# Experts of a mixture-of-experts block: whole steps of neighbouring pairs interleaved, TensorE's order of steps fixed

## The chip, the cores and the metric

The kernel runs on one core of a Trainium2 chip as one launch. The metric is the device time in microseconds (us) from its start to its end; lower is better.

## What is computed

The reference is two transformer blocks in a row on one sequence of 256 tokens with 1024 features, everything in float32. The first block (modulated norms, two kinds of attention, a convolutional feed-forward network) and the attention and convolution part of the second are not touched by the change. What it touches is the last part, a mixture of 32 experts in 4 groups of 8:

```python
y = jnp.zeros_like(h)
for g in range(G):
    hg = jnp.einsum('td,edf->tef', h, w_gate[g])
    hu = jnp.einsum('td,edf->tef', h, w_up[g])
    act = jax.nn.silu(hg) * hu * comb[:, g, :, None]
    y = y + jnp.einsum('tef,efd->td', act, w_down[g])
```

`comb` is zero but for the two experts that a token's router picks in the best group. An expert has a gate and an up matrix of 1024 x 512 and a down matrix of 512 x 1024, 6 MiB together, 192 MiB for all 32.

## The kernel before, in words

The experts are worked through in 16 pairs, by the loop at the end of `moe` (L1604). Each expert has 64 slots for tokens, a pair 128. For one pair the work on the engines is:

- choice: DVE builds `P` (tile `Pm`), a 0/1 matrix of tokens by slots (`onehot`, L1484).
- gather (L1493): TensorE multiplies the normed tokens `hn` by `P`; ScalarE (ACT) copies the result out of PSUM into `xg`. It is called twice for a pair, for half of the features each: once before `experts`, and once after the first quarter of the gate and up products.
- weights of the slots (L1513 to L1520): two small products with `carry`, then five small DVE operations, give `comb`; the choice turned round (L1523, L1525) gives `PTm`.
- gate and up (L1534): 64 matmul instructions, the two experts on the two halves of the array's columns; each fp32 product is two instructions. The weights `we` are loaded from HBM.
- `act` (L1540, L1541): Silu on ACT, then a product with the up result and `comb` on DVE.
- `act` turned (L1544): four transposes on TensorE; ACT copies the result to `aT` (L1546).
- down (L1563): 32 matmul instructions into two PSUM banks `py`, one for each half of the output columns.
- combination (`combine`, L1549): each half is split into a high part `yH` (ACT, L124) and a low part `yL` (DVE, L125); TensorE takes both back to the tokens with `PTm` (L1555, L1556), and DVE adds the result to `acc` (L1558).

The order in which each engine does these things is found by the program's scheduler when the program is built: it knows what depends on what and takes for each engine what is ready and comes earliest in the source. A tile gets a buffer when its first writer is scheduled, and gives it back after its last reader. The pool `tmp4` has two buffers for each tag; `act`, `aT` and `yH` share the tag `act`, and so share two buffers. `xg`, `yL` and `PTm` have one buffer each, `Pm` has two. PSUM is one pool of eight banks.

Weights come by DMA from SyncE's queue (SP, L1366; for the last pair's down matrices L1359), 1 MiB for one load, in the order of use (`eorder`, L1339), into some two dozen buffers that go round; a load starts when TensorE has done with what the buffer held. At the end `more_rounds` (L1635) repeats the work for experts with more than 64 tokens; with these inputs it runs zero times.

Of the kernel before, what the change touches and what calls it, by code (L numbers as in the profile page):

```python
# [20 lines left out]
S = 256  # L21
# [18 lines left out]
# no DMA starts on GpSimd: its ring of descriptors is left small  # L40
# [5 lines left out]
def make_consts():  # L46
# [42 lines left out]
    # for the first block only  # L89
# [14 lines left out]
class Builder:  # L104
# [45 lines left out]
    def wsplit(self, w, name="w"):  # L150
        """-> high and low part"""
        h, l = self.wpart(w.shape, name + "h"), self.wpart(w.shape, name + "l")
        self.split(w, h, l)
        return h, l

    def rsqrt(self, o, v, scale, tmp):
        # o = (v * scale + eps) ** -0.5
        self.nc.scalar.activation(tmp, v, AF.Ln, bias=self.eps[:tmp.shape[0]], scale=scale)
        self.nc.scalar.activation(o, tmp, AF.Exp, scale=-0.5)

    def table(self, name):
        """the set of activation functions for what follows"""
# [79 lines left out]
    def vecs(self):  # L242
        """small vectors, as columns over the partitions"""
# [79 lines left out]
        # -(e0 - e1 + init)  # L323
# [9 lines left out]
    def rope_tables(self):  # L333
# [12 lines left out]
        # wrap into [-pi, pi]  # L346
# [33 lines left out]
    def ada_half(self, pa, w, h):  # L380
        """four column blocks, each on its own columns of the array"""
# [8 lines left out]
    def ada_sum(self, ws):  # L390
        """four column blocks: the row chunks of ws, each times its part of silu(c), summed
        -> [128, 512], to be summed over the partitions"""
# [11 lines left out]
    def ada_ones(self, pa, a, stop=True):  # L404
        """the sum over the partitions, each column block on its own columns of the array"""
# [9 lines left out]
    def ada_cols(self, part):  # L415
        """rows -> columns [128, 4] in psum (without bias), in the order of the pairs"""
# [4 lines left out]
    def ada_load2(self, cols):  # L421
        """two column blocks"""
# [6 lines left out]
    def ada_first(self, w):  # L429
        """-> psum columns [128, 2]; a pair of row chunks on each part of the array"""  # L430
# [14 lines left out]
    def mixer(self):  # L445
# [5 lines left out]
        # small slices of w_in for the rope key and the forget gate, and their padded chunk  # L451
# [6 lines left out]
        # silu(c) as columns, 32 times over  # L458
# [13 lines left out]
        # rms of x, over all partitions  # L472
# [10 lines left out]
        # x, feature-major  # L483
# [41 lines left out]
        def ada(k):  # L525
            """scale and shift for chunks k, k + 1 of h; for one chunk if k < 2"""
# [86 lines left out]
        # --- fox q, k; latent q, kv: times gain, split; the row scale comes later  # L613
# [47 lines left out]
        # token-major sums for the value rows  # L661
# [3 lines left out]
        # --- forget gate, rope key  # L665
# [29 lines left out]
        # --- mla q, k, v  # L695
# [60 lines left out]
        # --- attention, with other products between its steps  # L756
# [23 lines left out]
        def values(kind, j, PT):  # L780
            """two heads, each on half of the array"""
# [14 lines left out]
        def gate(kind, n8):  # L796
            """a chunk of a gate"""
# [15 lines left out]
        # rest of adaLN: the mixer's gate; shift and scale of the ffn; its gate  # L813
# [3 lines left out]
        def ada_rest(n):  # L817
            """the sums over row chunks of four column blocks"""
# [16 lines left out]
        def out_prod(kind, i):  # L835
            """chunks 2i, 2i+1 of a branch's output"""
# [86 lines left out]
    def out_steps(self, wsrc, aH, aL, each, order=(0, 1, 2, 3)):  # L923
        """[D, D] product, feature-major; the last two k chunk by chunk, so that the results come one by one"""
# [17 lines left out]
    def softmax(self, sc):  # L942
        """psum scores [q, 384] (rows of the two query tiles) -> probabilities"""
# [12 lines left out]
    def turn_p(self, P):  # L956
        """blocks (q0,k0) (q1,k0) (q1,k1), turned"""
# [8 lines left out]
    def times_v(self, PTs, what):  # L966
        """o [n, 256] = v^T P^T, for each P and (v, column, n, o)"""
# [8 lines left out]
    def ffn_up(self, g):  # L976
        """parts of the weights of group g, gate and value"""
# [90 lines left out]
    def w2a_load(self, n):  # L1068
        """loads of the first n slices of w_in_2, columns of q, k, v"""
# [13 lines left out]
    def block2(self):  # L1083
# [6 lines left out]
        # sums for both norms; x2 * gains, split  # L1090
# [8 lines left out]
        def norms():  # L1099
# [9 lines left out]
            # eps / s_^2, for the sum over 64  # L1109
# [29 lines left out]
        # products out of psum  # L1139
# [9 lines left out]
        def group_sums(b):  # L1149
            """b [128, 2, S] -> sums of squares over groups of 64, in psum"""  # L1150
# [6 lines left out]
        def group_rms(pg, scaled):  # L1157
            """(mean square + eps / s_^2) ** -0.5, or without s_"""
# [9 lines left out]
        # convolution branch: xc, b, c  # L1168
# [26 lines left out]
        # row scale of v, token-major  # L1195
# [90 lines left out]
        def router(k):  # L1286
            """logits of groups and experts, and the sum of squares, feature by feature"""
# [5 lines left out]
        def router_w():  # L1293
            """router weights, times the gain of their norm"""
# [14 lines left out]
        for j in range(6):  # L1309
# [8 lines left out]
            if j == 2:  # L1318
                # output of the first block, the residual
# [31 lines left out]
    def prefetch(self, n):  # L1351
        for _ in range(n):
            e, nm, hf = key = self.eorder[self.enext]
            if nm == "down" and e == NE - 2:
                # for the last pair by halves of the columns, in turns
# [19 lines left out]
    def route(self):  # L1375
# [25 lines left out]
        # group: first largest, and its probability  # L1401
# [23 lines left out]
        e = self.e = col(2, 2)      # [tile, k]  # L1425
# [4 lines left out]
        # place of a token in its expert's list  # L1430
# [11 lines left out]
        rk = self.rk = col(2, 2)     # [tile, k], from 1  # L1442
# [5 lines left out]
        # weights of the two  # L1448
# [5 lines left out]
        def rest():  # L1454
# [5 lines left out]
            # w split, and the first choice, to be carried to the slots  # L1460
# [6 lines left out]
            # rounds beyond the first  # L1467
# [7 lines left out]
    def slots(self, u):  # L1475
        """u = 64 * expert + place if the place is in 1..64, else 0, of the places in rk"""
# [3 lines left out]
        # rk (rk - 65) is below zero for the places 1..64 only  # L1480
# [3 lines left out]
    def onehot(self, P, u, n):  # L1484
        """P [token, tile, slot]"""
# [7 lines left out]
    def gather(self, xg, P, n, half):  # L1493
        nc = self.nc
        mm = nc.tensor.matmul
        for cc in range(4 * half, 4 * half + 4, 2):
            b = self.bank((128, 2, n))
            for i in range(2):
                for t in range(2):
                    mm(b[:, i], self.hn[:, t, cc + i], P[:, t].bitcast(F32), start=(t == 0), stop=(t == 1),  # L1500
                       skip_group_check=True)
            nc.scalar.copy(xg[:, cc:cc + 2], b)  # L1502

    def experts(self, load, xg, P, first, acc, carry, each=None):
        """one pair of experts over 128 slots; adds to acc [token, tile, D].
        first: the pair's first expert, to compare with the carried one; each: what to do with a tile of
        tokens and half of the columns of acc, if the weights come by such halves"""
        nc, tmp, c = self.nc, self.tmp, self.c
        mm = nc.tensor.matmul
        # weight of a slot; slots to tokens  # L1510
        pw = self.bank()
        for t in range(2):
            mm(pw[:, 0:6], P[:, t], carry[:, t], start=(t == 0), stop=(t == 1))  # L1513
# [5 lines left out]
        comb = tmp.tile([128, 1], F32, name="comb")  # L1519
        nc.vector.scalar_tensor_tensor(a[:, 2:4], a[:, 0:2], 1.0, a[:, 5:7], op0=OP.mult, op1=OP.mult, accum_out=comb)  # L1520
        pp = self.bank((128, 2, 128), F32R)
        for t in range(2):
            nc.tensor.transpose(pp[:, t], P[:, t], self.identr)  # L1523
        PT = tmp.tile([128, 2, 128], F32R, name="PTm", bufs=1)
        nc.vector.tensor_copy(PT, pp.bitcast(F32))  # L1525
        ps = []
        for nm in ("gate", "up"):
            b = self.bank()
            for hf in range(2):
                w = [load(j, nm, hf) for j in range(2)]  # L1530
                for k in range(4):
                    kk = 4 * hf + k
                    for j in range(2):
                        mm(b[64 * j:64 * j + 64], xg[:, kk, 64 * j:64 * j + 64], w[j][:, k], start=(kk == 0),  # L1534
                           stop=(kk == 7), skip_group_check=True)
                if nm == "gate" and hf == 0:
                    self.gather(xg, P, 128, 1)
            ps.append(b)
        act = tmp.tile([128, 512], F32, name="act", tag="act")
        nc.scalar.activation(act, ps[0], AF.Silu)  # L1540
        nc.vector.scalar_tensor_tensor(act, ps[1], comb, act, op0=OP.mult, op1=OP.mult)  # L1541
        pt = self.bank((128, 4, 128))
        for f in range(4):
            nc.tensor.transpose(pt[:, f], act[:, f * 128:(f + 1) * 128], self.ident)  # L1544
        aT = tmp.tile([128, 4, 128], F32, name="aT", tag="act")
        nc.scalar.copy(aT, pt)  # L1546
        py = [self.bank() for _ in range(2)]

        def combine(n):  # L1549
            yH = tmp.tile([128, 512], F32R, name="yH", tag="act")  # L1550
            yL = tmp.tile([128, 512], F32R, name="yL", bufs=1)
# [128 lines left out]
```

## Time and profile before

| | |
|---|---|
| time, median of 3 runs | 1044.03 us (1042.81 to 1044.26) |
| span of the profiled execution, first to last instruction | 1041.6 us |
| time of that execution on its own | not given; the 2.4 us between the span and the median are taken as outside the span |
| mean granted TensorE clock | 0.993 |
| TensorE busy | 987.6 us, 95% |
| VectorE (DVE) busy | 515.3 us, 49% |
| ScalarE (ACT) busy | 371.9 us, 36% |
| experts' stage | from about 558 us to the end |

The span is the time between the first and the last instruction of one execution that the profiler recorded. Busy shares are means over stages with quite different limits. The chain of waits follows the work that ended last back to what released it. A TensorE row of the timeline counts to the modelled end of a matmul, so its rows overlap; the chain's rows do not.

### The profile page before, as it was taken

The numbers are of one execution on the slowest core, as the hardware profiler recorded it, in microseconds if no ns is written. First come the engines' busy times: TensorE is split into PE (matmuls) and PEld (weight loads), VectorE is DVE, ScalarE is ACT, GpSimd is POOL, SyncE is SP. The second block draws the span as 40 slices with busy tenths as digits, with TensorE's granted clock in tenths as the row PEclk, the third lists the DMA queues.
The fourth block names the chain that finished last, engine by engine and source line by source line (L and its number), as shares of the span: only waits on it lengthen the run. The fifth ranks groups of instructions, "written<-read, shape, count | busy, mean of one in ns | idle before, by whom it ended". The sixth has DMA issues, their size and how long they took to land.

```text
span 1041.6 us, 16242 instructions
## 1 busy us (share of the span) xinstructions
PE 987.6 (95%) x6676; PEld 709.1 (68%) x6676; DVE 515.3 (49%) x1004; ACT 371.9 (36%) x652; POOL 27.1 (3%) x25
## 2 busy tenths in 40 slices
PE   6999999999999999999998999999999999999996
PEld 5899999989999999898975443434444444344442
DVE  4868998759876675559744222112222222122121
ACT  3556656638554643656633111111111111111110
POOL 1010000010000000500000000000000000000000
PEclk8999999999999999999999999999999999999999
DMA  9977888539945555272859999999999999999901
GB/s 319 343 279 259 296 272 307 174 102 368 302 162 187 184 203 191 88 228 92 285 184 362 422 418 415 425 419 424 418 423 419 421 424 420 424 417 424 366 1 42
DMA packets 113350, 310.20 MB, mean 298 GB/s; under 512 B 9554, under 2 KB 59128, under 8 KB 96888
## 3 DMA queue, kind: packets, MB, share of 16 engines
q1 hardware_dynamic: 113182, 309.09, 78.1%
q8 instruction: 54, 0.88, 0.3%
q14 instruction: 24, 0.20, 0.1%
q10 hardware_dynamic: 90, 0.03, 0.0%
HBM read 308.05 MB, written 1.05 MB: 297 GB/s over the span
## 4 chain that ended last, share of the span: by engine, by line
PE 90%; DVE 4%; ACT 3%; issue 1%; DMA 0%; POOL 0%; SPq 0%; DVEq 0%; ACTq 0%; POOLq 0%
PE bank L1534 22%; PE bank L129 12%; PE bank L131 12%; PE bank L130 12%; PE bank L1563 11%; PE bank L1500 6%; PE bank L1555 2%; PE bank L1556 2%; DVE act L1541 1%; ACT wh L124 1%; PE bank L1544 1%; DVE wl L125 1%; ACT aT L1546 1%; PE g L129 1%; PE g L130 1%
## 5 line engine op out<-in xcount | busy, mean ns | idle before, releaser
L1534 PE MATMUL bank<-we,xg 128*64 128x512 f32 x1024 | 226.8, 595 | 0.0
L1534 PEld LDWEIGHTS bank<-we,xg 128*64 128x64 f32 x1024 | 70.7, 137 | 131.0 <-issue 127.3
L1563 PE MATMUL bank<-we,aT 128*64 128x512 f32 x512 | 115.1, 596 | 10.8 <-ACT aT L1546 10.8
L129 PE MATMUL bank<-fH,wh 128*128 128x256 f32 x352 | 99.5, 283 | 2.1 <-ACT fH L997 2.1
L130 PE MATMUL bank<-fL,wh 128*128 128x256 f32 x352 | 99.6, 283 | 0.0
L131 PE MATMUL bank<-fH,wl 128*128 128x256 f32 x352 | 99.5, 283 | 0.1
L1563 PEld LDWEIGHTS bank<-we,aT 128*64 128x64 f32 x512 | 38.9, 137 | 75.7 <-issue 60.5
L1541 DVE SCALAR_TENSOR_TENSOR act<-bank,comb,act 128x512 f32<-128x512 f32 x16 | 12.0, 751 | 157.1 <-PE bank L1534 157.1
L125 DVE TENSOR_TENSOR yL<-bank,yH 128x512 fp32r<-128x512 f32 x32 | 22.0, 688 | 131.7 <-ACT yH L124 131.7
L1500 PEld LDWEIGHTS bank<-Pm,hn 128*128 128x128 f32 x512 | 63.3, 192 | 15.6 <-issue 13.0
L1502 ACT COPY xg<-bank 128x256 f32<-128x256 f32 x64 | 23.9, 373 | 127.9 <-PE bank L1500 127.6
L129 PEld LDWEIGHTS bank<-fH,wh 128*128 128x128 f32 x352 | 67.5, 192 | 2.5 <-ACT fH L997 2.5
L131 PEld LDWEIGHTS bank<-fH,wl 128*128 128x128 f32 x352 | 67.5, 192 | 0.3 <-DVE wl L125 0.3
L130 PEld LDWEIGHTS bank<-fL,wh 128*128 128x128 f32 x352 | 67.6, 192 | 0.0
L1500 PE MATMUL bank<-Pm,hn 128*128 128x128 f32 x512 | 66.7, 278 | 0.0
L124 ACT CAST yH<-bank 128x512 fp32r<-128x512 f32 x32 | 18.8, 586 | 109.4 <-PE bank L1563 109.4
L125 DVE TENSOR_TENSOR wl<-wup,wh 128x2048 fp32r<-128x2048 f32 x22 | 50.3, 2289 | 10.6 <-ACT wh L124 10.6
L1546 ACT COPY aT<-bank 128x512 f32<-128x512 f32 x16 | 9.4, 586 | 125.4 <-PE bank L1544 125.4
L1558 DVE TENSOR_TENSOR acc<-acc,bank 128x512 f32<-128x512 f32 x64 | 41.1, 684 | 20.9 <-PE bank L1556 20.9
L130 PE MATMUL bank<-aL,wh 128*128 128x256 f32 x176 | 49.5, 283 | 0.0
L131 PE MATMUL bank<-aH,wl 128*128 128x256 f32 x176 | 49.5, 283 | 0.0
L129 PE MATMUL bank<-aH,wh 128*128 128x256 f32 x176 | 48.9, 283 | 0.0
(449 smaller groups left out, 2165.8 us busy)
## 6 DMA issues: line engine op xcount, KB each, us to landing
we<-in_w_exp_gate SPq DMA_DIRECT2D x64, 1024.0 KB
we<-in_w_exp_up SPq DMA_DIRECT2D x64, 1024.0 KB
we<-in_w_exp_down SPq DMA_DIRECT2D x60, 1024.0 KB
wup<-in_w_up SPq DMA_DIRECT2D x22, 1024.0 KB
wa<-in_w_ada SPq DMA_DIRECT2D x16, 1024.0 KB
wdn<-in_w_down SPq DMA_DIRECT2D x11, 1024.0 KB
wa<-in_w_ada SPq DMA_DIRECT2D x16, 512.0 KB
wgt<-in_w_in SPq DMA_DIRECT2D x8, 1024.0 KB
```

The source lines that it names most:

```text
L124: self.hi = self.nc.scalar.copy(hi, raw)
L125: self.nc.vector.tensor_sub(lo, raw, hi)
L129: mm(o, lh, rh, start=start, stop=False, skip_group_check=True)
L130: mm(o, lh, rl, start=False, stop=False, skip_group_check=True)
L131: return mm(o, ll, rh, start=False, stop=stop, skip_group_check=True)
L1500: mm(b[:, i], self.hn[:, t, cc + i], P[:, t].bitcast(F32), start=(t == 0), stop=(t == 1), skip_group_check=True)
L1502: nc.scalar.copy(xg[:, cc:cc + 2], b)
L1534: mm(b[64 * j:64 * j + 64], xg[:, kk, 64 * j:64 * j + 64], w[j][:, k], start=(kk == 0), stop=(kk == 7), skip_group_check=True)
L1541: nc.vector.scalar_tensor_tensor(act, ps[1], comb, act, op0=OP.mult, op1=OP.mult)
L1555: mm(b, PT[:, t], yH, start=True, stop=False)
L1558: nc.vector.tensor_add(o, o, b)
L1563: mm(py[n][64 * j:64 * j + 64], aT[:, ff, 64 * j:64 * j + 64], w, start=(ff == 0), stop=(ff == 3), skip_group_check=True)
```

## The change

The function `experts`, which did a whole pair, is cut into steps: `gate_up`, `weigh` (weights of the slots), `activate`, `turn_act`, `down`, `parts` (the split of one half), `combine` (one half) and `back` (the choice turned round). The gather of a pair becomes one step, `cols`. The loop then runs through the steps of two neighbouring pairs: gate and up of pair p; the whole gather of pair p+1; the first half of the combination of pair p-1; the transposes of pair p; the weights of the slots of pair p+1; the second half of the combination of pair p-1; the choice of pair p turned round; down of pair p. `step` puts each TensorE instruction of a step behind the last one of the step before (`issue_after`); the other engines' order is left to the scheduler. In `down` the last four products run by halves of the columns, so that the first bank is complete sooner. `combine` takes both high parts, then both low parts. For the last pair the first half is combined between the down products. The rest of the diff takes comments out, and `more_rounds` calls the new functions one after the other.

```diff
-    def gather(self, xg, P, n, half):
+    def gather(self, P):
...
-        for cc in range(4 * half, 4 * half + 4, 2):
-            b = self.bank((128, 2, n))
+        xg = self.tmp.tile([128, KD, 128], F32, name="xg", bufs=1)
+        for cc in range(0, KD, 2):
+            b = self.bank((128, 2, 128))
...
-                if nm == "gate" and hf == 0:
-                    self.gather(xg, P, 128, 1)
...
+    def activate(self, pair):
+        nc = self.nc
+        act = pair["act"] = self.tmp.tile([128, 512], F32, name="act", tag="act")
+        pg, pu = pair.pop("ps")
+        nc.scalar.activation(act, pg, AF.Silu)
+        nc.vector.scalar_tensor_tensor(act, pu, pair["comb"], act, op0=OP.mult, op1=OP.mult)
...
+        pair["aT"] = self.tmp.tile([128, 4, 128], F32, name="aT", tag="act")
+        nc.scalar.copy(pair["aT"], pt)
...
+                        f, n = (i // 2, i % 2) if hf == 0 else (i % 2, i // 2)
+                        last = one(2 * hf + f, n, j, w[j][:, f, n * 512:(n + 1) * 512])
...
+    def parts(self, pair, n):
+        yH = self.tmp.tile([128, 512], F32R, name="yH", tag="act")
+        yL = self.tmp.tile([128, 512], F32R, name="yL", bufs=1)
+        self.split(pair["py"][n], yH, yL)
+        pair[n] = yH, yL
+
+    def combine(self, pair, n, each=None):
+
+        nc, PT, acc = self.nc, pair["PT"], self.acc
+        if n not in pair:
+            self.parts(pair, n)
+        bs = [self.bank() for _ in range(2)]
+        for i, y in enumerate(pair.pop(n)):
+            for t in range(2):
+                last = nc.tensor.matmul(bs[t], PT[:, t], y, start=(i == 0), stop=(i == 1))
+        for t in range(2):
+            o = acc[:, t, n * 512:(n + 1) * 512]
+            nc.vector.tensor_add(o, o, bs[t])
...
+        def step(f, *a):
+
+            with ExitStack() as st:
+                if at[0]:
+                    st.enter_context(tc.issue_after(at[0].ins))
+                at[0] = f(*a)
...
-        for p in range(NE // 2):
-            pair(p, store if p == NE // 2 - 1 else None)
+        select(0)
+        step(cols, 0)
+        self.route_rest()
+        for p in range(np_):
+            q, last = pairs[p], p == np_ - 1
+            load = lambda j, nm, hf: self.expert_w(2 * p + j, nm, hf)
+            if not last:
+                select(p + 1)
+            step(self.gate_up, q, load)
+            if p == 0:
+                step(self.weigh, q, 0)
+            self.activate(q)
+            if p:
+                self.parts(pairs[p - 1], 0)
+            if not last:
+                step(cols, p + 1)
+            if p:
+                step(self.combine, pairs[p - 1], 0)
+            step(self.turn_act, q)
+            if not last:
+                step(self.weigh, pairs[p + 1], 2 * p + 2)
+            if p:
+                step(self.combine, pairs.pop(p - 1), 1)
+            step(self.back, q)
+            if last:
+                def halves(n, i, mm):
+                    at[0] = mm
+                    if n and i == 0:
+                        step(self.combine, q, 0, store)
+                    if i:
+                        self.parts(q, n)
+                step(self.down, q, load, halves)
+                step(self.combine, q, 1, store)
+            else:
+                step(self.down, q, load)
```

## Rows read from the trace of the kernel before

**Rows 1.** The page: TensorE's busy time and share; the chain's shares by engine.

```profile
PE 987.6 (95%) x6676; PEld 709.1 (68%) x6676; DVE 515.3 (49%) x1004; ACT 371.9 (36%) x652; POOL 27.1 (3%) x25
...
PE 90%; DVE 4%; ACT 3%; issue 1%; DMA 0%; POOL 0%; SPq 0%; DVEq 0%; ACTq 0%; POOLq 0%
```

**Rows 2.** Chain of waits through pair 14: start us, us, what.

```profile
974.88 3.58 PE bank L1534 x16
978.47 1.98 PE bank L1500 x16
980.45 10.47 PE bank L1534 x48
991.00 0.76 DVE act L1541
991.81 0.67 PE bank L1544 x4
992.50 0.59 ACT aT L1546
993.14 7.14 PE bank L1563 x32
1000.28 0.66 PE bank L1555 x2
1000.94 0.61 PE bank L1556 x2
1001.55 0.47 PE bank L1555 x2
1002.02 1.56 PE bank L1500 x14
1003.58 0.47 PE bank L1556 x2
1004.05 0.22 PE bank L1500 x2
1004.27 0.12 PE bank L1513 x2
1004.39 0.22 PE bank L1523 x2
1004.61 3.58 PE bank L1534 x16
```

**Rows 3.** Chain of waits: first gate products of the first and the second pair.

```profile
558.54 3.58 PE bank L1534 x16
...
588.26 3.58 PE bank L1534 x16
```

**Rows 4.** Waits from 600 to 1041 us: total us, times, longest.

```profile
PE bank L1544 <- DVE act L1541: 14.2, 15, 1.0
...
PE bank L1563 <- ACT aT L1546: 10.1, 15, 0.7
```

**Rows 5.** Timeline: ACT and DVE work of the combination and the Silu.

```profile
999.46 0.59 ACT L124 CAST yH<-bank 128x512 fp32r<-128x512 f32 x1 [6.37 <-PE bank L1563]
...
1000.07 0.69 DVE L125 TENSOR_TENSOR yL<-bank,yH 128x512 fp32r<-128x512 f32 x1 [8.32 <-ACT yH L124]
...
1001.36 1.29 DVE L1558 TENSOR_TENSOR acc<-acc,bank 128x512 f32<-128x512 f32 x2 [0.59 <-PE bank L1556]
...
1013.81 0.60 ACT L1540 ACTIVATE act<-bank 128x512 f32<-128x512 f32 x1 [3.22 <-PE bank L1534]
```

**Rows 6.** Timeline: issue of the last loads, and the last down products.

```profile
967.51 12.37 SPq L1359 DMA_DIRECT2D we<-in_w_exp_down  x8
...
1030.50 1.94 PE L1563 MATMUL bank<-we,aT 128*64 128x512 f32 x8
```

**Rows 7.** Windows: length, PE, PEld, DVE, ACT, POOL, clock, DMA share, GB/s.

```profile
919.44:949.19 29.75, 28.12 (x147) 12.97 (x146) 6.78 (x18) 3.85 (x8) 0.00 (x0) 1.00 1.02 420
...
979.90:990.00 10.10, 10.10 (x51) 3.70 (x52) 0.00 (x0) 1.03 (x3) 0.00 (x0) 1.00 0.74 273
```

More of the change, by code (lines that the diff above doesn't have):

```diff
@@ L1491, in onehot, with weigh @@
             nc.vector.scalar_tensor_tensor(P[:, t], io, u[:, t, 1:2], p1, op0=OP.is_equal, op1=OP.add)
-    def gather(self, xg, P, n, half):
+    def gather(self, P):
         nc = self.nc
-        mm = nc.tensor.matmul
-        for cc in range(4 * half, 4 * half + 4, 2):
-            b = self.bank((128, 2, n))
+        xg = self.tmp.tile([128, KD, 128], F32, name="xg", bufs=1)
+        for cc in range(0, KD, 2):
+            b = self.bank((128, 2, 128))
             for i in range(2):
                 for t in range(2):
-                    mm(b[:, i], self.hn[:, t, cc + i], P[:, t].bitcast(F32), start=(t == 0), stop=(t == 1),
-                       skip_group_check=True)
+                    last = nc.tensor.matmul(b[:, i], self.hn[:, t, cc + i], P[:, t].bitcast(F32), start=(t == 0),
+                                            stop=(t == 1), skip_group_check=True)
             nc.scalar.copy(xg[:, cc:cc + 2], b)
-    def experts(self, load, xg, P, first, acc, carry, each=None):
-        nc, tmp, c = self.nc, self.tmp, self.c
-        mm = nc.tensor.matmul
+        return xg, last
+    def weigh(self, pair, first):
+        nc, tmp, c, P = self.nc, self.tmp, self.c, pair["P"]
         pw = self.bank()
         for t in range(2):
-            mm(pw[:, 0:6], P[:, t], carry[:, t], start=(t == 0), stop=(t == 1))
+            last = nc.tensor.matmul(pw[:, 0:6], P[:, t], self.carry[:, t], start=(t == 0), stop=(t == 1))
         a = tmp.tile([128, 8], F32, name="cw")
@@ L1518, in experts, with back, gate_up @@
         nc.vector.tensor_scalar(a[:, 6:7], a[:, 4:5], float(-first), c["eslot"], op0=OP.add, op1=OP.not_equal)
-        comb = tmp.tile([128, 1], F32, name="comb")
-        nc.vector.scalar_tensor_tensor(a[:, 2:4], a[:, 0:2], 1.0, a[:, 5:7], op0=OP.mult, op1=OP.mult, accum_out=comb)
+        pair["comb"] = tmp.tile([128, 1], F32, name="comb")
+        nc.vector.scalar_tensor_tensor(a[:, 2:4], a[:, 0:2], 1.0, a[:, 5:7], op0=OP.mult, op1=OP.mult,
+                                       accum_out=pair["comb"])
+        return last
+    def back(self, pair):
+        nc, P = self.nc, pair["P"]
         pp = self.bank((128, 2, 128), F32R)
         for t in range(2):
[L1523 to L1526, printed above, removed]
+            last = nc.tensor.transpose(pp[:, t], P[:, t], self.identr)
+        pair["PT"] = self.tmp.tile([128, 2, 128], F32R, name="PTm", bufs=1)
+        nc.vector.tensor_copy(pair["PT"], pp.bitcast(F32))
+        return last
+    def gate_up(self, pair, load):
+        mm = self.nc.tensor.matmul
+        pair["ps"] = []
         for nm in ("gate", "up"):
@@ L1533, in experts @@
                     for j in range(2):
-                        mm(b[64 * j:64 * j + 64], xg[:, kk, 64 * j:64 * j + 64], w[j][:, k], start=(kk == 0),
-                           stop=(kk == 7), skip_group_check=True)
-                if nm == "gate" and hf == 0:
-                    self.gather(xg, P, 128, 1)
[L1538 to L1541, printed above, removed]
+                        last = mm(b[64 * j:64 * j + 64], pair["xg"][:, kk, 64 * j:64 * j + 64], w[j][:, k],
+                                  start=(kk == 0), stop=(kk == 7), skip_group_check=True)
@@ L1542, in experts, with turn_act @@
+            pair["ps"].append(b)
+        return last
+    def activate(self, pair):
[4 more added lines that the diff above has]
+        nc.vector.scalar_tensor_tensor(act, pu, pair["comb"], act, op0=OP.mult, op1=OP.mult)
+    def turn_act(self, pair):
+        nc, act = self.nc, pair.pop("act")
         pt = self.bank((128, 4, 128))
         for f in range(4):
-            nc.tensor.transpose(pt[:, f], act[:, f * 128:(f + 1) * 128], self.ident)
@@ L1545, in experts @@
[L1545 to L1551, printed above, removed]
-            self.split(py[n], yH, yL)
-            for t in range(2):
-                b = self.bank()
-                mm(b, PT[:, t], yH, start=True, stop=False)
-                mm(b, PT[:, t], yL, start=False, stop=True)
-                o = acc[:, t, n * 512:(n + 1) * 512]
-                nc.vector.tensor_add(o, o, b)
-                if each:
-                    each(t, n)
@@ L1562, in down, with one @@
-        def down(ff, n, j, w):
-            mm(py[n][64 * j:64 * j + 64], aT[:, ff, 64 * j:64 * j + 64], w, start=(ff == 0), stop=(ff == 3),
-               skip_group_check=True)
+            last = nc.tensor.transpose(pt[:, f], act[:, f * 128:(f + 1) * 128], self.ident)
+        pair["aT"] = self.tmp.tile([128, 4, 128], F32, name="aT", tag="act")
+        nc.scalar.copy(pair["aT"], pt)
+        return last
+    def down(self, pair, load, halves=None):
+        aT, py = pair["aT"], [self.bank() for _ in range(2)]
+        pair["py"] = py
+        def one(ff, n, j, w):
+            return self.nc.tensor.matmul(py[n][64 * j:64 * j + 64], aT[:, ff, 64 * j:64 * j + 64], w, start=(ff == 0),
+                                         stop=(ff == 3), skip_group_check=True)
@@ L1566, in experts @@
         for hf in range(2):
             w = [load(j, "down", hf) for j in range(2)]
-            if each:
-                for ff in range(4):
-                    for j in range(2):
-                        down(ff, hf, j, w[j][:, ff])
-                continue
-            for f in range(2):
-                for n in range(2):
-                    for j in range(2):
-                        down(2 * hf + f, n, j, w[j][:, f, n * 512:(n + 1) * 512])
-        for n in range(2):
-            combine(n)
+            for i in range(4):
+                for j in range(2):
+                    if halves:
+                        last = one(i, hf, j, w[j][:, i])
+                    else:
+                        f, n = (i // 2, i % 2) if hf == 0 else (i % 2, i // 2)
+                        last = one(2 * hf + f, n, j, w[j][:, f, n * 512:(n + 1) * 512])
+                if halves and i % 2:
+                    halves(hf, i // 2, last)
@@ new lines, in down @@
+        return last
+    def parts(self, pair, n):
[14 more added lines that the diff above has]
+            nc.vector.tensor_add(o, o, bs[t])
+            if each:
+                each(t, n)
+        return last
@@ L1614, in moe, with select @@
         self.prefetch(NW + NS + NN + 1)
-        def pair(p, each=None):
+        np_ = NE // 2
+        pairs = {}
+        def select(p):
             u = tmp.tile([128, 2, 2], F32, name="ug")
@@ L1620, in pair, with cols @@
             self.onehot(P, u, 128)
-            xg = tmp.tile([128, KD, 128], F32, name="xg", bufs=1)
-            self.gather(xg, P, 128, 0)
-            if p == 0:
-                self.route_rest()
-            self.experts(lambda j, nm, hf: self.expert_w(2 * p + j, nm, hf), xg, P, 2 * p, acc, self.carry, each)
+            pairs[p] = {"P": P}
+        at = [None]
+        def step(f, *a):
[3 more added lines that the diff above has]
+                at[0] = f(*a)
+        def cols(p):
+            pairs[p]["xg"], last = self.gather(pairs[p]["P"])
+            return last
         out = self.out.rearrange("o (t p) d -> (o p) t d", p=128)
@@ L1630, in store @@
             nc.sync.dma_start(out[:, t, 512 * n:512 * n + 512], acc[:, t, 512 * n:512 * n + 512])
-        for p in range(NE // 2):
-            pair(p, store if p == NE // 2 - 1 else None)
+        select(0)
[31 more added lines that the diff above has]
+                step(self.combine, q, 1, store)
+            else:
+                step(self.down, q, load)
         self.more_rounds(store)
@@ L1648, in more_rounds @@
                 self.onehot(P, u, 128)
-                xg = tmp.tile([128, KD, 128], F32, name="xg", bufs=1)
-                self.gather(xg, P, 128, 0)
+                q = {"P": P, "xg": self.gather(P)[0]}
                 def load(j, nm, hf):
@@ L1656, in load @@
                     return w
-                self.experts(load, xg, P, 0, acc, carry)
+                self.weigh(q, 0)
+                self.gate_up(q, load)
+                self.activate(q)
+                self.turn_act(q)
+                self.down(q, load)
+                self.back(q)
+                for n in range(2):
+                    self.combine(q, n)
                 nc.vector.tensor_scalar_add(u, u, -128.0)
```

## The prediction

> **What bounds the kernel now.** I read the page first: TensorE (PE) is busy for 95% of the span and carries 90% of the chain of waits [rows 1]. That looks as if nothing could be had, but a share is a mean, so I went to the chain of one expert pair, which is the stretch that the change rewrites. From one pair's first gate product to the next pair's is 29.73 us, 974.88 to 1004.61 [rows 2], and the 14 pairs from 588.26 to 1004.61 take 29.74 us each [rows 2, 3]. In it the reader should find four places where PE does not stream. After the gate and up products end at 990.92 the chain goes through VectorE (DVE, `act`) and PE starts again at 991.81: 0.89 us. After the four transposes it goes through ScalarE (ACT, `aT`), 992.48 to 993.14: 0.66 us. The four transposes take 0.67 us although two like ones (L1523) take 0.22 us in the stream, so 0.44 us would do: 0.23 us. The first half of the combination takes 0.66 + 0.61 us where the second half, whose inputs are ready, takes 0.47 + 0.47: 0.33 us. The waits of PE confirm the first two: 14.2 us and 10.1 us over 15 pairs, and nothing longer stands there [rows 4]; PE never waits for a load in this stage.
>
> So PE's own sequence bounds the stage, with 0.89 + 0.66 + 0.23 + 0.33 = 2.11 us a pair that isn't streaming. The profile gives a span of 1041.6 us and no separate time for that execution; the median of the runs is 1044.03 us, so I make the sum against the span and add 2.4 us at the end.
>
> **The change, part by part.** Moved without a price of their own: the gather's two halves become one (1.98 + 1.56 + 0.22 = 3.76 us before and after), the slot weights (0.12 us) and the transposes of the choice (0.22 us) change place [rows 2]. The choice itself on DVE comes earlier, beside the gate products, where DVE has nothing else to do; if that cover went, PE would wait about one DVE operation for it, 0.7 us by `yL` [rows 5]. No load is moved past another on SP's queue: `eorder` and the cycle of slots are the same, a load only starts when PE lets go of a slot sooner. The new order of the eight down products (0.22 us each at 7.14 us for 32 instructions) lets the first output bank finish sooner; it costs nothing in itself.
>
> Removed, if everything is ready when PE asks: `act` now has the gather and half a combination (3.76 + 0.94 us) to hide its 0.60 + 0.76 us; `aT` (0.59 us) has 0.12 + 0.94 + 0.22 us; the first half of the parts, `yH` and `yL` (0.59 + 0.69 us [rows 5]), has a whole gate and up stretch of 3.58 + 10.47 us. All four losses go, and a pair takes 29.73 - 2.11 = 27.62 us. That is one end, a gain of 2.11 us a pair.
>
> **The wait that comes instead.** The tiles `act`, `aT` and both `yH` share one tag in a pool of two buffers (L1525, L1540, L1546 and the new `parts`). In the old order two were enough, since a pair finished its `yH` before the next pair's `act`. Now the combination of pair p-1 lies on both sides of pair p's transposes, and three of these tiles are wanted at about one time. The change fixes PE's order only; which tile takes the free buffer is left to the program's scheduler. I see two orders, and price both from the same rows [rows 2, 5].
>
> (A) `act` of pair p gets its buffer during the gate products; the second `yH` gets none before the transposes have read `act`. Behind the last transpose: 0.23 us until its result is out, 0.02 + 0.59 us `aT`, 0.02 + 0.59 us `yH`, 0.04 us to PE: 1.49 us, of which the slot weights hide 0.12 us: 1.37 us idle. `yL` ends another 0.69 us after `yH`, PE takes it up about 0.06 us later, and the `yH` products cover 0.47 us: 0.26 us more. Together 1.63 us; a pair takes 27.62 + 1.63 = 29.25 us.
>
> (B) The second `yH` takes the buffer as soon as `aT` of the pair before is done with, and `act` waits until the first half of the combination has read the first `yH`. From that half's start: 0.66 us for the two `yH` products, 0.04 + 0.60 us for the Silu [rows 5], DVE meanwhile in its first addition from about 1.01 to 1.66 us (0.54 us behind the `yL` products' start, 1.29 us for two), then 0.76 us for `act`, transposes at about 2.48 us against 0.94 us without a wait: 1.54 us. The second addition and `yL` come after `act`, and the `yL` products wait 0.33 us for them. Together 1.87 us; a pair takes 29.49 us. Behind the waiting Silu stand only copies that PE does not want yet; PE itself is who waits.
>
> The other end of this unknown wait is (C) below, 2.85 us. I take A and B, because the two-buffer tag is in the code and both ways round it stalls, and they lie close together.
>
> **The sum.** The first gate product now starts at 558.54 [rows 3]. It moves back by the other half of the gather, 1.78 us, less the weights and transposes that move behind it, 0.34 us: 560.0. The first pair has no combination to do: 14.05 + 0.12 + 3.76 + 0.44 + 0.12 + 0.22 + 7.14 = 25.85 us, to 585.85 (588.26 now [rows 3]). Fourteen pairs follow: by A 14 x 29.25 = 409.5 us, to 995.4. The last pair has no gather and no next weights (29.25 - 3.76 = 25.49 us with the cover of 0.12 us gone) and 0.94 us of its own combination between its down products: 26.4 us, to 1021.8. Now the last down product ends at 1030.50 + 1.94 = 1032.44 [rows 6]. What is behind it stays. A: 10.6 us less, a span of 1031.0 and a time of 1033.4. B by the same working: 998.7, 1025.4, 7.0 us less, a time of 1037. My forecast is 1034 us, faster by 1%; its own range is 1027 to 1042 us.
>
> **Are the loads in the way?** Every pair needs 12 loads of 1 MiB, 12.58 MB. In one pair's time the DMA engines are fully busy and move 420 GB/s [rows 7], which makes 29.95 us a pair, no less than PE takes now. The Trainium skill, HBM Reference, section Specifications (TRN2), says that a core streaming alone comes to about 425 GB/s, bounded by its DMA engines; 12.58 MB at that rate is an estimate of 29.6 us a pair, by which the stage could not get shorter and the time would stay near 1044. The rows speak against it: the last eight loads are issued from 967.51 on [rows 6] and the traffic ends inside the stretch to 990.0 (273 GB/s mean, 0.74 busy) [rows 7], while PE uses the last of them at 1030.50 [rows 6]. PE is some 40 us behind the loads. So the transfers hold the end to about 990 + 1.9 + 9.2 us (last products and tail) = 1001 us, not to 1044, and all the gain of A, B and even of the full 2.11 us fits into the lead.
>
> **The rivals.** *Full gain*: the scheduler finds an order in which the second `yH` takes the first one's buffer right at the combination, and nothing stalls. Then 585.85 + 14 x 27.62 = 972.5, the last pair 27.62 - 3.88 + 0.94 = 24.7 us, 997.2: 35.2 us less, 1008.8 us. For it: PE's order gives each step enough cover. Against: two buffers. *Slower* (C): as B, but DVE takes both additions and `yL` ahead of `act`: 1.01 + 1.29 + 0.69 + 0.76 + 0.04 = 3.79 us from the half's start, a wait of 2.85 us. A pair then takes 30.47 us; 560.0 + 25.85 + 14 x 30.47 = 1012.4, the last pair 27.7 us, 1040.1: 7.7 us more, 1051.7 us. It decides as soon as the new wait is over some 2.3 us (2.11 us a pair and the first pair's 2.4 us spread over 14). For it: DVE takes its work in one order, and two of these are ready before the Silu ends. Against: `act` comes earlier in the program. *Loads bind*: as weighed above, no change, 1044 us; it needs the lead to be gone, and the rows show 40 us of it.
>
> **How the numbers follow.** A change under 0.2% (about 2 us) can't be told from none here. A or B 0.50, full gain 0.25, slower 0.17, loads bind 0.08. A small part of B's spread reaches no change or above. So faster 0.75, same 0.09, slower 0.16. The range takes in A, B, the full gain with some 4 us for the unseen edges, and no change: 1005 to 1046 us; it leaves out nearly all of C.
>
> **What would show it.** Right: the waits of PE for `act` and `aT` gone or nearly; the gather in one piece of about 3.8 us; a pair of about 29.3 us; a new wait of PE for `yH` (A) or for `act` with the Silu behind the combination (B), 1.4 to 1.9 us. Full gain: no wait of PE over 0.2 us and pairs of 27.6 us. C: transposes waiting over 2.3 us. Loads: PE waiting for `we`. I would be wrong if the first half of the combination kept its 1.27 us, or if the gather or the transposes cost more in their new places than the rows of before say.

## The result and the profile after

The changed kernel takes 1024.16 us (median of 4 runs, 1023.10 to 1024.95) against 1044.07 us for the kernel before (4 runs): a ratio of 0.9815, 95% interval 0.9801 to 0.9828, 19.9 us less. The forecast was 1034 us with a range of 1005 to 1046. So the direction was right and the time lies in the range, 10 us below the forecast. It lies outside the narrower range of 1027 to 1042 us that went with cases A and B; the wide range holds it because it takes in the full gain.

On the page of the changed kernel TensorE (PE) and the chain look almost as before [rows 1]:

```profile
PE 978.9 (96%) x6676; PEld 707.6 (69%) x6676; DVE 515.2 (50%) x1004; ACT 368.8 (36%) x652; POOL 27.1 (3%) x25
...
PE 92%; ACT 3%; DVE 2%; DMA 1%; issue 1%; POOL 0%; SPq 0%; DVEq 0%; ACTq 0%; POOLq 0%
```

A share can't show the change: the same instructions are there in a shorter time. The chain of waits through one pair does; these are its pieces (start us, us, what), and they answer to [rows 2]:

```profile
815.49 13.73 PE bank L1544 x64
829.23 3.77 PE bank L1501 x32
833.00 0.93 PE bank L1601 x4
833.92 0.45 PE bank L1560 x4
...
834.40 0.59 ACT aT L1562
834.98 0.50 ACT yH L124
...
835.52 1.47 PE bank L1601 x4
836.99 0.12 PE bank L1529 x2
837.12 7.02 PE bank L1571 x32
844.13 1.28 PE bank L1544 x5
```

A pair takes 844.13 - 815.49 = 28.64 us instead of 29.73 us. The reader should see four things. The product on VectorE (DVE) for `act` is no longer on the chain. `aT` still is, but not because the down products wait for it: ScalarE (ACT) does `aT` and then the second `yH`, and it is the second half of the combination (L1601 at 835.52) that waits for that `yH`. The four transposes take 0.45 us and not 0.67 us. And the 64 gate and up products take 13.73 us in one piece, where they were 3.58 + 10.47 = 14.05 us.

The waits of PE from 600 us to the end (total us, times, longest) say the same; the two lines of [rows 4], 24.3 us together, are gone, and one of 16.5 us stands in their place:

```profile
PE bank L1601 <- ACT yH L124: 16.5, 16, 1.2
```

On the timeline of ACT and DVE (start, us, engine, line, operation) the order is that of case A in the prediction: `aT` first, the second `yH` behind it, `yL` behind that:

```profile
834.40 0.59 ACT L1562 COPY aT<-bank 128x512 f32<-128x512 f32 x1 [0.99 <-PE bank L1560]
834.88 0.59 ACT L124 CAST yH<-bank 128x512 fp32r<-128x512 f32 x1
...
835.50 0.69 DVE L125 TENSOR_TENSOR yL<-bank,yH 128x512 fp32r<-128x512 f32 x1
...
835.52 0.73 PE L1601 MATMUL bank<-yH,PTm 128*128 128x512 f32 x2 [1.04 <-ACT yH L124]
```

The loads end where they ended before. In the windows of [rows 7] (length, PE, PEld, DVE, ACT, POOL, clock, DMA share, GB/s) one pair's DMA is as busy as it was, and the traffic still ends at about 990; but PE now uses the last load at 1011.69 and not at 1030.50 [rows 6]:

```profile
815.49:844.13 28.64, 27.60 (x147) 12.70 (x144) 6.84 (x19) 3.64 (x8) 0.00 (x0) 1.00 1.02 425
...
979.50:990.00 10.50, 10.50 (x50) 3.86 (x52) 1.62 (x3) 0.00 (x0) 0.00 (x0) 1.00 0.83 306
```

```profile
1011.69 1.94 PE L1571 MATMUL bank<-we,aT 128*64 128x512 f32 x8
```

PE's lag behind the loads fell from some 40 us to some 22 us.

### The profile page after: what moved, and what is told of

It is laid out like the page before. It is cut to its first block, busy times and chain, and to the rows that moved or that the text cites. A ratio compares the mean times of both kernels' runs of the same rounds, so it can differ in the third digit from the quotient of the medians.

```text
span 1022.8 us, 16189 instructions
## 1 busy us (share of the span) xinstructions
PE 978.9 (96%) x6676; PEld 707.6 (69%) x6676; DVE 515.2 (50%) x1004; ACT 368.8 (36%) x652; POOL 27.1 (3%) x25
## 4 chain that ended last, share of the span: by engine, by line
PE 92%; ACT 3%; DVE 2%; DMA 1%; issue 1%; POOL 0%; SPq 0%; DVEq 0%; ACTq 0%; POOLq 0%
PE bank L1544 21%; PE bank L129 13%; PE bank L130 13%; PE bank L131 13%; PE bank L1571 11%; PE bank L1501 6%; PE bank L1601 4%; ACT aT L1562 1%; PE g L129 1%; ACT yH L124 1%; PE g L130 1%; PE g L131 1%; PE bank L1560 1%; ACT wh L124 1%; PE bank L970 1%; PE bank L961 1%
## 5 line engine op out<-in xcount | busy, mean ns | idle before, releaser
L1544 PE MATMUL bank<-we,xg 128*64 128x512 f32 x1024 | 222.5, 592 | 0.0
L1544 PEld LDWEIGHTS bank<-we,xg 128*64 128x64 f32 x1024 | 73.5, 137 | 145.7 <-issue 144.4
L1553 ACT ACTIVATE act<-bank 128x512 f32<-128x512 f32 x16 | 9.6, 597 | 237.7 <-PE bank L1544 237.7
L1571 PEld LDWEIGHTS bank<-we,aT 128*64 128x64 f32 x512 | 35.3, 137 | 65.3 <-issue 63.5
L1501 PEld LDWEIGHTS bank<-Pm,hn 128*128 128x128 f32 x512 | 59.4, 195 | 11.5 <-issue 11.5
L1501 PE MATMUL bank<-Pm,hn 128*128 128x128 f32 x512 | 62.4, 281 | 0.0
L124 ACT CAST wh<-wup 128x2048 fp32r<-128x2048 f32 x22 | 41.8, 1902 | 14.0 <-PE bank L130 13.3
```

The costliest lines, as they stand in the source:

```text
L124: self.hi = self.nc.scalar.copy(hi, raw)
L1501: last = nc.tensor.matmul(b[:, i], self.hn[:, t, cc + i], P[:, t].bitcast(F32), start=(t == 0), stop=(t == 1), skip_group_check=True)
L1544: last = mm(b[64 * j:64 * j + 64], pair["xg"][:, kk, 64 * j:64 * j + 64], w[j][:, k], start=(kk == 0), stop=(kk == 7), skip_group_check=True)
L1571: return self.nc.tensor.matmul(py[n][64 * j:64 * j + 64], aT[:, ff, 64 * j:64 * j + 64], w, start=(ff == 0), stop=(ff == 3), skip_group_ch ...
```

## The experiments

The theory after the result: the change hides `act`, `aT` and the breaks between products of different shape, and pays for it with a wait for the second `yH`, which has no buffer until the transposes have read `act`. Its rivals: the wait is ScalarE's serial work whatever the buffers; the gain comes from the combination's place, or from the fixed order as such; the loads set the end. All runs below are compared with the kernel before on the same chip; its medians there were 1043.8 and 1043.7 us.

**Sharing the two buffers out differently.**

```diff
-        act = pair["act"] = self.tmp.tile([128, 512], F32, name="act", tag="act")
+        act = pair["act"] = self.tmp.tile([128, 512], F32, name="act", tag="act", bufs=1)
...
-        yH = self.tmp.tile([128, 512], F32R, name="yH", tag="act")
+        yH = self.tmp.tile([128, 512], F32R, name="yH", tag="yH", bufs=1)
```

(`aT` has the tag `act` with one buffer too, and two small tiles of the router are given one tag each.)

> The changed kernel with the same memory shared out differently: act and aT share one buffer, yH has one of its own, instead of all three sharing two. The second yH can then start when the first half of the combination has read the first one, before the transposes. Buffer theory: the 1.04 us for which TensorE waits for the second yH in each pair goes; but yL then stands behind two additions on VectorE (1.29 us) and becomes what TensorE waits for, some 0.6 us, so a pair takes about 28.2 us against 28.64, and the time falls by 5 to 7 us to about 1018. Rival (the wait is ScalarE's serial work, aT then yH, whatever the buffers): the wait stays at 1.0 us and the time at 1024.

Measured: 1016.79 us (1016.39 to 1017.41), ratio 0.9742 (0.9726 to 0.9758). With the same memory the wait for `yH` is gone but for one in the last pair; what is left is a wait for `yL`, 0.7 us a time. The chain of one pair shows why (start us, us, what): `yL` stands behind the two additions of the first half.

```profile
880.73 3.77 PE bank L1501 x32
884.50 0.72 PE bank L1601 x3
...
885.24 1.28 DVE acc L1604 x2
...
886.60 0.61 DVE yL L125
...
887.25 0.73 PE bank L1601 x2
```

A pair takes 895.12 - 866.99 = 28.13 us. So it was the buffer: ACT's work is the same and PE no longer waits for it.

**The gather behind the transposes.**

```diff
-            if not last:
-                step(cols, p + 1)
             if p:
                 step(self.combine, pairs[p - 1], 0)
             step(self.turn_act, q)
             if not last:
+                step(cols, p + 1)
                 step(self.weigh, pairs[p + 1], 2 * p + 2)
```

> The changed kernel with two steps exchanged and no more memory: the first half of the combination stands right behind the gate and up products, then the transposes, then the whole gather of the next pair, then the rest. The gather (3.77 us) then covers aT, the second yH and its yL. Buffer theory: no wait of TensorE over 0.2 us is left, a pair takes 13.73 + 0.94 + 0.45 + 3.77 + 0.12 + 0.94 + 0.22 + 7.02 = 27.2 us, the time falls by about 14 x 1.4 + 1 = 20 us to 1004. Loads theory: the last load lands at 990 in both kernels, so the end can't come before about 1001, and TensorE begins to wait for weights in the last pairs; then 1004 to 1010. Rival (the steps cost more in other places): 1015 or more.

Measured: 1007.60 us (1007.49 to 1010.00), ratio 0.9661 (0.9645 to 0.9677). This beats both kernels, the changed one by 16.6 us. Its chain through one pair has nothing but PE in it (two short steps of 0.12 us are left out here):

```profile
805.38 13.73 PE bank L1544 x64
819.11 1.13 PE bank L1601 x4
820.24 0.44 PE bank L1560 x4
820.68 3.57 PE bank L1501 x32
...
824.37 1.04 PE bank L1601 x4
...
825.53 7.02 PE bank L1571 x32
832.55 1.71 PE bank L1544 x7
```

A pair takes 832.55 - 805.38 = 27.17 us, as expected. The time is 3.6 us above my 1004, inside what the loads theory allowed, but 1.5 us of that are not the loads: the first pair takes 588.10 - 560.50 = 27.60 us against 26.08 us in the changed kernel, since it has no combination and no gather ahead of its transposes, and PE waits 1.8 us for its `act`. The last pair has no gather, so there PE waits 1.16 us for the second `yH` again, and it waits for weights for the first time in this stage (from the timeline, the last 14 up products of the last pair):

```profile
980.36 3.65 PE L1544 MATMUL bank<-we,xg 128*64 128x512 f32 x14 [0.81 <-DMA we<-in_w_exp_up]
...
986.74 0.73 PE L1601 MATMUL bank<-yH,PTm 128*128 128x512 f32 x2 [1.16 <-ACT yH L124]
```

**The order left to the scheduler.**

```diff
         def step(f, *a):
 
             with ExitStack() as st:
-                if at[0]:
-                    st.enter_context(tc.issue_after(at[0].ins))
                 at[0] = f(*a)
```

> The changed kernel with the same steps in the source, but TensorE's order left to the program's scheduler. If the fixed order is what brings the gain, this comes back towards 1044; if the order of the source is enough, it stays within 5 us of 1024. In the first pairs the scheduler keeps the steps and only puts two down products into the wait for yL (0.26 us), in later ones it mixes gate products and the gather, which costs up to 0.3 us for each break. I expect 1022 to 1030.

Measured: 1075.5 us (1075.18 to 1078.6), ratio 1.0303 (1.0286 to 1.0320). I expected 1022 to 1030 and missed by 45 us; it is slower than the kernel before. Its first pairs take about 29.57 us (615.97 to 645.54), where the scheduler put two down products into the wait for `yL`; from the seventh on a pair takes 33.8 to 33.9 us, but for two that take 32.3 us. The chain of the seventh (734.24 to 768.14, 33.90 us), cut:

```profile
734.24 6.87 PE bank L1544 x33
741.11 2.65 PE bank L1501 x22
743.76 3.58 PE bank L1544 x14
747.34 0.64 PE bank L1501 x4
747.98 1.00 PE bank L1544 x2
...
754.40 0.76 DVE act L1554
...
757.90 1.75 PE bank L1571 x2
759.65 1.15 PE bank L1601 x2
760.80 6.91 PE bank L1571 x29
```

Gate products and gather are cut into each other, so the products take longer and `act` has no cover left. And two down products that take 0.43 us in a stream take 1.75 us; in the first pairs, at full clock, the same two take 1.00 us. The window 758 to 760 shows TensorE's granted clock at 0.50, that is 1.2 GHz, after PE was busy for 1.14 and 0.97 us in the two windows of 2 us before:

```profile
754.00:756.00 2.00, 1.14 (x7) 0.69 (x6) 0.75 (x1) 1.30 (x5) 0.00 (x0) 1.00 1.05 434
756.00:758.00 2.00, 0.97 (x5) 0.76 (x6) 1.50 (x8) 0.97 (x2) 0.00 (x0) 1.00 1.01 418
758.00:760.00 2.00, 2.00 (x3) 0.44 (x3) 1.21 (x4) 0.00 (x0) 0.00 (x0) 0.50 0.99 410
760.00:762.00 2.00, 2.00 (x8) 0.55 (x9) 1.59 (x4) 0.00 (x0) 0.00 (x0) 0.64 1.05 438
```

Over the pairs of 33.8 to 33.9 us the mean clock is 0.95. The two pairs of 32.3 us (802.04 to 834.36 and 1003.61 to 1035.93) have the same order and a clock of 1.00 throughout. So the cut order costs 32.3 - 29.57 = 2.7 us a pair, and the clock another 1.5 us where it falls. In the changed kernel the clock is 1.00 in all 16 pairs. So the fixed order is a needed part of the change, not a detail: without it the same steps lose 51 us.

**The gather whole, in the kernel before.**

```diff
-                if nm == "gate" and hf == 0:
-                    self.gather(xg, P, 128, 1)
...
             self.gather(xg, P, 128, 0)
+            self.gather(xg, P, 128, 1)
```

> The kernel before with only the gather made whole, ahead of the pair's gate and up products. It measures the price of breaking the 64 gate and up products into 16 and 48, which the prediction took as nothing: 3.58 + 10.47 = 14.05 us against 13.73 in the changed kernel. If the break costs 0.32 us, a pair takes 29.4 us and the time falls by 5 us to 1039; if the 0.32 us come from something else, it stays within 2 us of 1044.

Measured: 1038.04 us (1037.31 to 1038.23), ratio 0.9946 (0.9929 to 0.9962). A pair gets shorter by what I expected: in the chain it takes 882.87 - 853.47 = 29.40 us against 29.73 us. But only 0.12 us of the 0.33 us are in the gate and up products (13.93 us); 0.19 us are in the gather, 1.56 + 2.01 = 3.57 us and not 3.76 us:

```profile
853.47 13.93 PE bank L1534 x64
...
878.50 1.56 PE bank L1500 x14
...
880.52 2.01 PE bank L1500 x18
```

**The combination back in its own pair.**

```diff
-            if p:
-                step(self.combine, pairs[p - 1], 0)
             step(self.turn_act, q)
...
                 step(self.down, q, load)
+                step(self.combine, q, 0)
+                step(self.combine, pairs.pop(p), 1)
```

> The changed kernel with one part undone: a pair's combination stands behind its own down products again, in the fixed order gate and up, gather of the next pair, transposes, weights of the slots, choice turned round, down, both halves of the combination. Buffer theory: carrying the combination into the next pair is what calls for the third buffer, so without it the 1.04 us wait for the second yH goes; what is left is about 0.5 us for aT behind the transposes and 0.2 us for the last yL, a pair of about 28.3 us and a time of 1017 to 1021, faster than the change itself. Rival (interleaving the combination is what brings the gain, because it hides yH and yL): the pair goes to 29.2 us or more and the time to 1032 or more.

Measured: 1038.28 us (1037.87 to 1040.40), ratio 0.9954 (0.9938 to 0.9971). My expectation fails, and the rival's is met: a pair takes 855.23 - 825.61 = 29.62 us. The wait for `yH` does go, as the buffer theory says, but I had taken the second `yL` to run before the additions. In the chain DVE does additions of the first half first, as in the first experiment, and PE waits for `yL` longer than it did for `yH`; 0.34 us a pair for `aT` come to it. From the waits of PE (total us, times, longest):

```profile
PE bank L1601 <- DVE yL L125: 17.9, 14, 1.3
```

So carrying the combination into the next pair is worth 29.62 - 28.64 = 0.98 us a pair, even though it brings a wait of 1.04 us with it. About 0.27 us of this are streams that start behind products of another shape again (gate and up 13.88 us against 13.73 us, down 7.14 us against 7.02 us).

**The order of the last down products.**

```diff
-                        f, n = (i // 2, i % 2) if hf == 0 else (i % 2, i // 2)
+                        f, n = i // 2, i % 2
```

> The changed kernel with only the order of the last four down products put back, so that the first output bank is complete 0.43 us before the end of the down products and not 0.86 us. The prediction took the new order at nothing. In the changed kernel the first yH is not started before the Silu of the next pair, 7 us later, so nothing waits for that bank: within 2 us of 1024. If the earlier bank matters, 1 to 6 us slower.

Measured: 1024.58 us (1023.29 to 1025.22), ratio 0.9815 (0.9798 to 0.9831): no difference from the change. That part is worth nothing here.

**Less work for TensorE in the fastest version.** The low parts of the experts' output are left out, so the result is less exact.

```diff
-        yL = self.tmp.tile([128, 512], F32R, name="yL", bufs=1)
-        self.split(pair["py"][n], yH, yL)
-        pair[n] = yH, yL
+        self.nc.scalar.copy(yH, pair["py"][n])
+        pair[n] = yH,
```

> The kernel with the gather behind the transposes, with the low parts of the experts' output left out: no yL on VectorE, and four of the eight combination products of a pair go. TensorE's work falls by 0.94 us a pair, 15 us over the stage. Loads theory: the loads run at their ceiling of 12.58 MB in 29.8 us and land at about 990 whatever TensorE does, so nearly all of the 15 us is spent waiting for weights, and the time is 1003 to 1007. If the loads do not bind yet, it falls to about 993.

Measured: 1006.03 us (1005.03 to 1007.24), ratio 0.9638 (0.9622 to 0.9654). The time falls by 1.6 us and lies where the loads theory put it, but its premise of 15 us fails. A pair takes 883.44 - 856.69 = 26.75 us against 27.17 us, which is 5.9 us over 14 pairs: the first half of the combination is now too short to hide `act`, so that the chain goes through DVE again (here the pair from 910 on), and the transposes take 0.66 us and not 0.44 us.

```profile
925.74 0.76 DVE act L1554
...
926.55 0.66 PE bank L1560 x4
```

The traffic still ends at about 990, and TensorE waits for weights five times:

```profile
PE bank L1544 <- DMA we<-in_w_exp_up: 4.3, 5, 1.4
```

So some 4 of the 5.9 us go into waits for weights. PE takes up the last 14 up products of the last pair at 981.61 us here and at 980.36 us with the gather behind the transposes, although it has less to do here. So from the gather behind the transposes on, the loads set the end; there they have just begun to, with one wait of 0.81 us.

**Both improvements together** (the own buffer for `yH` and the gather behind the transposes, the first two diffs).

> The gather behind the transposes and a buffer of its own for yH together. In the pairs up to the last one no wait is left that the buffer could take away. In the last pair, which has no gather to cover it, TensorE waits 1.16 us for the second yH; with its own buffer that yH starts before the transposes. So 0.5 to 1 us less at the most, 1006 to 1008, and nothing if the loads set the end.

Measured: 1008.87 us (1007.86 to 1010.41), ratio 0.9669 (0.9653 to 0.9685), the same as the gather behind the transposes alone. Here too PE waits for the last pair's up weights (the last 14 up products start at 982.36 us). In the last pair the wait for `yH` before the second half of the combination is traded for one of 0.8 us for `yL`.

## Why the prediction was right, and where it was off

*The bound and the four losses.* Right. PE's own sequence bounded the stage, and the waits for `act` and `aT` and the longer transposes went, and the first half of the combination takes 0.93 us and not 1.27 us, as the trace of before said.

*The moved parts at no price.* Right for the choice and for the order of the down products (the experiment that undid it: no difference). Wrong for what making the gather whole does to the products around it: I took 3.76 us for the gather and 3.58 + 10.47 us for the gate and up products, before and after. The gather does take 3.77 us, but the gate and up products take 13.73 us. A change between products on half the array's columns and products on all of them costs 0.1 to 0.2 us: the gather takes 3.57 us behind the transposes and 3.77 us behind the gate and up products, and the first half of the combination takes 0.93 us behind the gather and 1.13 us behind the gate and up products. The order before had six such changes in a pair, the new one has two. That is 0.32 us a pair that the sum lacked. The gather made whole in the old kernel removes two changes and gives 0.33 us, but only 0.12 us of it in the gate and up products (13.93 us). The other 0.20 us go where these products now stand behind the down products, which use half of the columns too; in the first pair, behind the gather, they take 13.88 us.

*The wait that comes instead.* The mechanism was right, case A: two buffers for three tiles, `aT` before `yH`, one wait of PE for `yH`. The first experiment shows the cause, since the same memory shared out differently takes that wait away. Its size came out about right, in part by luck: from the transposes' result to the end of the second half I had 1.26 + 0.47 + 0.26 + 0.47 = 2.46 us, and the chain shows 836.99 - 834.38 = 2.61 us. PE's wait for `yH` by itself is 1.04 us, where I had 1.37 us and named 1.4 to 1.9 us as the sign: the transposes' result is out right behind them and not 0.23 us later, and ACT starts `yH` 0.11 us before `aT` ends. The second half behind it takes 1.47 us, where I had 1.20 us. The two errors nearly cancel. Case B, `act` waiting for the buffer, did not come, and so case C, which stood on it, had no ground.

*The sum.* The mis-sized terms are the streams: 29.25 us was predicted for a pair and 28.64 us measured. The gate and up products are 0.32 us shorter, the down products 0.12 us, the transposes with their result 0.22 us, the choice turned round 0.10 us; what follows the transposes' result is 0.15 us longer. That is 0.61 us a pair, and the 14 full pairs take 400.9 us and not 409.5 us. The first gate products and the first pair were together 0.6 us later than the sum had it (586.42 against 585.85), in part since `aT` of the first pair has no combination to hide behind; the last pair was right, 26.36 us against 26.4 us. So the span is 8.2 us below case A's (1022.8 us against 1031.0 us). The time is 1 us further off, because the 2.4 us that I added for what lies outside the span were too much: it is 1.8 us in the profiled run, which itself took 0.4 us more than the median. I had read durations off rows where each stream starts behind a wait or a change of shape, and kept that start in the new order.

*The loads.* Right for the changed kernel: PE had 40 us of lead to use up, and the loads did not bind. The rule of the Trainium skill (HBM Reference, section Specifications (TRN2)) of about 425 GB/s for a core that streams alone agrees with the 418 to 425 GB/s of the changed kernel's pairs from 586 to 959 us (425 GB/s in the one above). What the loads mean for the end shows in the faster versions: with lead left over they cost nothing, and at 1006 to 1009 us they hold the time. The bound in the prediction, a span of 1001 us, was some 5 us too low, because it looked at the last load alone. The load that PE waits for is an earlier one, of the last pair's up weights: its products start at 980.36 us in the version with the gather behind the transposes, and 25 us of PE's work follow, to a span of 1005.7 us.

*Full gain.* I gave it 0.25 and 1008.8 us. It did not come with this order of steps; the order with the gather behind the transposes reaches 27.17 us a pair and 1007.6 us.

## What to carry to other kernels

When work of two tiles is interleaved, count the buffers that are alive at the same time, and put the longest independent step right behind the one whose result goes through another engine: moving one step was worth 16.6 us here, nearly as much as the whole change (19.9 us). Sum a new order from streams in the middle of a run, and price each change of the array's shape by itself. Before the gain is taken as open-ended, look where the loads end, at each load of the last tiles and not only at the last one; here the lead was 40 us, and with 36 us gained PE had begun to wait for weights.

## What was not expected of the hardware

The weight loads of TensorE (PEld) stand idle for 0.81 us before the first full-array load behind products on half the columns; before a load inside the stream on half the columns it is 0.28 us (changed kernel, first line inside the stream, second at the gather):

```profile
828.20 0.14 PEld L1544 LDWEIGHTS bank<-we,xg 128*64 128x64 f32 x2 [0.28 <-issue]
829.16 3.65 PEld L1501 LDWEIGHTS bank<-Pm,hn 128*128 128x128 f32 x32 [0.81 <-issue]
```

So filling a short wait with products of another shape can cost more than the wait: the free order put two down products into a wait for `yL`, and its pairs took 29.57 us and not 28.64 us, at full clock. And in its seventh pair a stretch of 4 us in which TensorE was busy for 2.11 us (754 to 758) was followed by 2 us at a mean granted clock of 0.50 and 2 us at 0.64. In its ninth pair TensorE was busy for 2.11 us of 4 us too (822 to 826), and the clock stayed at 1.00; what makes the difference is not shown. The waits of 1.04 us in the changed kernel never led to a fall of the clock.
